# Rotated attention scores as products over 64 rows, one head in each half of the array

## The chip, the cores and the metric

The kernel runs on one core of a Trainium2 chip. The metric is the device time of one launch in microseconds; lower is better. The time before is the median of 3 runs, 2278.76 us (2278.57 to 2279.04).

## What is computed

A trunk of two layers over 256 tokens of width 2048, in float32: latent attention (MLA), a wide MLP, a state-space mixer (SSM), and a second MLP. The change lies in the attention scores. Each of the 16 heads has queries and keys of 192 numbers: 128 that are used as they are and 64 that are rotated by the token's position. The rotated part of the keys is the same for all heads up to a factor.

```
q = concatenate([q[..., :128], apply_rope(q[..., 128:], cos, sin)])
k = concatenate([k[..., :128], apply_rope(k[..., 128:], cos, sin)])
s = einsum('bqhd,bkhd->bhqk', q_blk, k) * 192 ** -0.5     # per block of 128 queries
p = softmax(where(k_pos <= q_pos, s, -inf))
o = einsum('bhqk,bkhd->bqhd', p, v)
```

So a score is a sum over 192 products: 128 of the unrotated part and 64 of the rotated one.

## The kernel before

**Stages.** `trunk` runs `mla`, `mlp`, `ssm`, `mlp` one after another. Nearly all of the time is projections: weights come from HBM in pieces of 128x1024 (queue of SP, line 85), ScalarE rounds a piece to float32r (L102), VectorE takes the rest (L103), and PE multiplies both halves (L340, L341, L344 in `block`; L619 to L621 in the MLPs). The weights are split three pieces ahead of PE.

**Units.** The 16 heads are worked on two at a time, in 8 units u. PE's order is the order of the calls in `mla_body` (PE alone is scheduled by hand; the other engines' order is set by a planner when the kernel is built). For each u, in that order:

- `s0q(u+1)`: the projection to the queries of the next unit
- `s1(u-1, "k")`: the normed keys of the unit before, transposed by PE (L940, L942) into two banks, then copied out into `kT`
- `s0kv(u)`: the projection to keys and values, with `s3(u-2)` in the middle, which transposes the softmax's result
- `s2(u-1)`: the scores of both heads (PE, L964 and L965), the masked copy with the maximum (VectorE, L968), the exponentials (ScalarE, L974), and the division
- `s4(u-2)`: scores times values (L1000, L1001), split by ScalarE and VectorE (L300, L301)
- `s1(u, "q")`: the normed queries, transposed into `qT`

In the last units the output projection (`wob`) takes the place of the projections that are not left.

**The layout of the scores' operands.** `kT` has three slabs of 128 rows: the unrotated keys of head 0, of head 1, and in slab 2 the rotated keys of head 0 in rows 0 to 63 and of head 1 in rows 64 to 127. `qT` has four: slabs 0 and 1 are the unrotated queries, slab 2 holds head 0's rotated queries in rows 0 to 63 with zeros below, slab 3 head 1's in rows 64 to 127 with zeros above. POOL writes the zeros (L930, L931), ScalarE the halves (L947). With the zeros, a product over all 128 rows of slab 2 of `kT` picks out one head.

**The scores.** Per head there are two blocks of queries: the first 128 queries against 128 keys, the other 128 against 256. Each is one product with the unrotated slab (L964) and one with the rotated slab (L965), summed in PSUM, in columns 0 to 127 and 128 to 383 of one bank per head. Plain float32 products run as two passes on PE, each with a weight load of its own.

**Banks.** `bank()` hands out four PSUM banks in rotation (two of pool `yp`, two of pool `sm`); a bank is written again when its readers are done.

**POOL** also computes the roots of the norms (L290, L291), the rotation (L801 to L804) and issues a copying DMA (L900).

Of the kernel before, what the change touches and what calls it, by code (L numbers as in the profile page):

```python
# [28 lines left out]
P = 128  # L29
# [186 lines left out]
class Trunk:  # L216
# [612 lines left out]
    def mla_body(self, mp, gain):  # L829
        nc, d = self.nc, self.d  # L830
# [93 lines left out]
        def s1(u, name):  # L924


            src, words = U[u][name + "n"], U[u].get(name + "w")
            dst = self.ktile(self.xtp, F32)
            if name == "q":
                nc.gpsimd.memset(dst[64:128, 2], 0.0)  # L930
                nc.gpsimd.memset(dst[0:64, 3], 0.0)  # L931
            for i in range(2):
                b = self.bank()
                parts = 2 - i
                for j in range(parts):
                    for t in range(2):
                        o = j * 256 + t * P
                        k = (2 * i + j) * P
                        if words is not None and (i, t) != (1, 1):
                            nc.tensor.transpose(b.bitcast(F32R)[:, o:o + P], words[:, t, k:k + P], self.ident_r)  # L940
                        else:
                            nc.tensor.transpose(b[:, o:o + P], src[:, t, k:k + P], self.ident)  # L942
                v = b[:, :parts * 256].rearrange("p (k n) -> p k n", k=parts)
                if i and name == "q":
                    for h in range(2):
                        r = slice(64 * h, 64 * h + 64)
                        nc.scalar.activation(dst[r, 2 + h], b[r, 0:256], AF.Copy)  # L947
                elif (i == 0) == (name == "q"):
                    nc.vector.tensor_copy(dst[:, 2 * i:2 * i + parts], v)
                else:  # L950
                    nc.scalar.activation(dst[:, 2 * i:2 * i + parts], v, AF.Copy)
            U[u][name + "T"] = dst

        def s2(u):
            qT, kT = U[u]["qT"], U[u]["kT"]
            p = self.ktile(self.xtp, F32).rearrange("p a b -> p (a b)")
            mx, nm, sm, rc = self.stat(4), self.stat(4), self.stat(4), self.stat(4)
            spans = ((0, P), (P, 384))
            for h in range(2):
                b = self.bank()  # L960
                q0, q1 = qT[:, h], qT[:, 2 + h]
                k0, k1 = kT[:, h], kT[:, 2]
                for o, n in ((0, P), (P, 256)):
                    nc.tensor.matmul(b[:, o:o + n], q0[:, o:o + P], k0[:, :n], start=True, stop=False)  # L964
                    nc.tensor.matmul(b[:, o:o + n], q1[:, o:o + P], k1[:, :n], start=False, stop=True)  # L965
                for i, (a, z) in enumerate(spans):
                    j = 2 * h + i
                    nc.vector.tensor_tensor_reduce(p[:, h * 384 + a:h * 384 + z], b[:, a:z], mk[:, 256 - (z - a):], 1.0, -3.0e38,  # L968
                                                   ALU.add, ALU.max, mx[:, j:j + 1])
                nc.vector.tensor_scalar(nm[:, 2 * h:2 * h + 2], mx[:, 2 * h:2 * h + 2], -SCALE, None, ALU.mult)  # L970
                for i, (a, z) in enumerate(spans):
                    j = 2 * h + i
                    v = p[:, h * 384 + a:h * 384 + z]
                    nc.scalar.activation(v, v, AF.Exp, bias=nm[:, j:j + 1], scale=SCALE, accum_out=sm[:, j:j + 1])  # L974
                nc.vector.reciprocal(rc[:, 2 * h:2 * h + 2], sm[:, 2 * h:2 * h + 2])
                for i, (a, z) in enumerate(spans):
                    j = 2 * h + i
                    nc.vector.tensor_scalar(p[:, h * 384 + a:h * 384 + z], p[:, h * 384 + a:h * 384 + z], rc[:, j:j + 1],
                                            None, ALU.mult)
            U[u]["p"] = p  # L980
# [40 lines left out]
        for u in range(UNITS):  # L1021
            if 0 < u and u + 1 < UNITS:
                s0q(u + 1)
                q_stats(u + 1)
            if u == UNITS - 1:
                a0 = wob(0, 0)
            if u >= 1:
                s1(u - 1, "k")
            if 0 < u and u + 1 < UNITS:
                q_norm(u + 1)  # L1030
            s0kv(u, (lambda: s3(u - 2)) if u >= 2 else None)
            if u + 1 < UNITS:
                q_rope(u + 1, self.pow.ins)
            if u == UNITS - 1:
                k_norm(u)
            if u >= 1:
                s2(u - 1)
            if u >= 2:
                s4(u - 2)
            s1(u, "q")  # L1040
            if u < UNITS - 1:
                k_norm(u)
        self.boundary_begin(gain, True)
        a1 = wob(1, 0)
        s1(UNITS - 1, "k")
        s3(UNITS - 2)
        wob(0, 1, a0)
        s4(UNITS - 2)
        s2(UNITS - 1)
        wob(1, 1, a1)  # L1050
        s3(UNITS - 1)
# [758 lines left out]
```

## Time and profile before

| | before |
|---|---|
| median of 3 runs | 2278.76 us |
| the profiled execution, its own time | 2280.22 us |
| its span, first to last instruction | 2278.4 us |
| PE busy | 2267.4 us |
| VectorE (DVE) busy | 1965.4 us |
| ScalarE (ACT) busy | 1441.1 us |
| GpSimd (POOL) busy | 285.1 us |
| granted TensorE clock | 1.00 |

The span is shorter than the execution's own time by 1.8 us of start and end. PE's matmuls are pipelined: a row's length holds the tail of a pass that overlaps the next one, so what a pass costs is the distance from its start to the next start. Attention takes the span from about 0 to 280 us; the eight units lie between about 66 and 212 us.

### The profile page before, as it was taken

How to read it: one execution, taken by the hardware profiler on the slowest of the kernel's cores; microseconds unless marked ns; L12 is line 12 of the kernel's file. 1: busy time of each engine (PE TensorE's matmuls, PEld its weight loads, DVE VectorE, ACT ScalarE, POOL GpSimd, SP SyncE). 2: the span in 40 equal slices, each digit the busy share in tenths (PEclk: the TensorE clock that was granted, in tenths of full speed). 3: DMA queues.
4: the chain of work that ended last, by engine and by line, in shares of the span. 5: the costliest groups of instructions: out<-in, count | busy, mean ns of one | idle time of the engine just before them, and what ended most of it. 6: DMA issues, size and time to landing. Idle time of an engine off the chain costs nothing.

```text
span 2278.4 us, 30856 instructions
## 1 busy us (share of the span) xinstructions
PE 2267.4 (100%) x10881; PEld 1880.1 (83%) x10881; DVE 1965.4 (86%) x2257; ACT 1441.1 (63%) x2044; POOL 285.1 (13%) x339
## 2 busy tenths in 40 slices
PE   9999999999999999999999999999999999999999
PEld 7898888888888888888888788888888888887887
DVE  7786697998999897879989998976989989989985
ACT  6775476566666566566677676565666665665663
POOL 1440000000000000100002532230000000000000
PEclk9999999999999999999999999999999999999999
DMA  8545678888888877768898889877788888898875
GB/s 316 174 153 151 218 229 264 255 260 267 265 254 262 270 240 241 237 195 260 274 366 285 291 293 330 268 227 221 219 256 251 258 275 244 259 280 238 265 230 162
DMA packets 176026, 569.74 MB, mean 250 GB/s; under 512 B 20192, under 2 KB 29344, under 8 KB 175872
## 3 DMA queue, kind: packets, MB, share of 16 engines
q1 hardware_dynamic: 147808, 498.24, 65.2%
q0 software_dynamic: 16320, 56.88, 11.7%
q10 hardware_dynamic: 11744, 12.66, 1.8%
q8 instruction: 85, 1.39, 0.2%
q14 instruction: 69, 0.57, 0.1%
HBM read 542.23 MB, written 6.41 MB: 241 GB/s over the span
## 4 chain that ended last, share of the span: by engine, by line
PE 94%; DVE 2%; DMA 2%; ACT 1%; issue 1%; POOL 0%; SPq 0%; ACTq 0%; DVEq 0%
PE acc L340 11%; PE acc L341 11%; PE acc L344 11%; PE yp L621 9%; PE yp L620 9%; PE yp L619 9%; PE st L620 7%; PE st L621 7%; PE st L619 7%; DMA wraw<-mi 1%; PE st L1162 1%; PE st L1163 1%; PE st L1164 1%; DVE wl L103 1%; PE yp L340 1%; PE yp L341 1%
## 5 line engine op out<-in xcount | busy, mean ns | idle before, releaser
L102 ACT ACTIVATE wh<-wraw 128x1024 fp32r<-128x1024 f32 (+1 forms) x818 | 857.4, 1053 | 526.3 <-PE acc L341 187.4
L103 DVE TENSOR_TENSOR wl<-wraw,wh 128x1024 fp32r<-128x1024 f32 (+1 forms) x818 | 989.1, 1227 | 180.2 <-ACT wh L102 171.0
L619 PE MATMUL yp<-wh,k 128*128 128x512 f32 x896 | 349.3, 390 | 0.0
L621 PE MATMUL yp<-wh,k 128*128 128x512 f32 x896 | 348.8, 389 | 0.0
L620 PE MATMUL yp<-wl,k 128*128 128x512 f32 x896 | 348.6, 389 | 0.0
L102 ACT ACTIVATE wh<-wrx 128x1024 fp32r<-128x1024 f32 x192 | 203.2, 1058 | 167.6 <-PE yp L621 104.4
L103 DVE TENSOR_TENSOR wl<-wrx,wh 128x1024 fp32r<-128x1024 f32 x192 | 233.6, 1222 | 39.4 <-ACT wh L102 37.6
L621 PEld LDWEIGHTS yp<-wh,k 128*128 128x128 f32 x896 | 168.2, 188 | 35.1
L620 PEld LDWEIGHTS yp<-wl,k 128*128 128x128 f32 x896 | 168.2, 188 | 34.9
L619 PEld LDWEIGHTS yp<-wh,k 128*128 128x128 f32 x896 | 168.2, 188 | 34.8
L340 PE MATMUL acc<-wh,k 128*128 128x512 f32 x496 | 196.4, 396 | 0.0
L341 PE MATMUL acc<-wh,k 128*128 128x512 f32 x496 | 193.4, 390 | 0.0
L340 PE MATMUL acc<-wh,xt 128*128 128x512 f32 x480 | 191.8, 400 | 1.2 <-ACT wh L102 1.2
L341 PE MATMUL acc<-wh,xt 128*128 128x512 f32 x480 | 187.4, 390 | 0.5 <-DVE xt L484 0.4
L619 PE MATMUL st<-wh,xt 128*128 128x512 f32 x448 | 177.7, 397 | 0.0
L621 PE MATMUL st<-wh,xt 128*128 128x512 f32 x448 | 174.9, 390 | 0.0
L620 PE MATMUL st<-wl,xt 128*128 128x512 f32 x448 | 174.7, 390 | 0.0
L200 POOL DMA_DIRECT2D wrx<-mi x56 | 49.0, 875 | 724.3 <-DVE wl L103 513.4
L619 PE MATMUL st<-wh,sN 128*128 128x512 f32 x336 | 133.2, 396 | 0.4 <-ACT wh L102 0.4
L620 PE MATMUL st<-wl,sN 128*128 128x512 f32 x336 | 131.5, 391 | 1.9 <-DVE wl L103 1.8
L344 PE MATMUL acc<-wl,k 128*128 128x512 f32 x496 | 132.7, 389 | 0.0
L621 PE MATMUL st<-wh,sN 128*128 128x512 f32 x336 | 131.1, 390 | 0.0
(342 smaller groups left out, 3808.6 us busy)
## 6 DMA issues: line engine op xcount, KB each, us to landing
wraw<-mi SPq DMA_DIRECT2D x256, 512.0 KB, 5.6
wraw<-mo SPq DMA_DIRECT2D x256, 512.0 KB, 5.4
wraw<-si SPq DMA_DIRECT2D x160, 512.0 KB, 6.0
wraw<-so SPq DMA_DIRECT2D x64, 512.0 KB, 4.9
wrx<-mi SPq DMA_DIRECT2D x56, 512.0 KB, 5.2
wrx<-mi POOLq DMA_DIRECT2D x56, 512.0 KB, 7.5
wraw<-wo SPq DMA_DIRECT2D x32, 512.0 KB, 4.0
tap<-xD SPq DMA_DIRECT2D x24, 512.0 KB, 8.1
```

Of the source, the lines that this page charges most:

```text
L102: self.last = nc.scalar.activation(h[:, v], raw[:, v], AF.Copy)
L103: self.last_lo = nc.vector.tensor_tensor(lo[:, v], raw[:, v], h[:, v].bitcast(F32), ALU.subtract)
L200: nc.gpsimd.dma_start(st["b11"].tile, quarter(d, 1, 0), accum_op=ALU.add)
L340: nc.tensor.matmul(accs[t][:, :n], ah, wh[:, q, :], start=first and kt + q == 0, stop=False)
L341: nc.tensor.matmul(accs[t][:, :n], al, wh[:, q, :], start=False, stop=False)
L344: nc.tensor.matmul(accs[t][:, :n], lhs(kt + q, t)[0], wl[:, q, :], start=False, stop=en and q == nk - 1)
L619: nc.tensor.matmul(b, ah, wh, start=first and q == 0, stop=False)
L620: nc.tensor.matmul(b, ah, wl, start=False, stop=False)
L621: nc.tensor.matmul(b, al, wh, start=False, stop=last and q == 1)
L1162: nc.tensor.matmul(bank[onto], ah, wh, start=done + q == 0 and not skip, stop=False, skip_group_check=skip)
L1163: nc.tensor.matmul(bank[onto], al, wh, start=False, stop=False, skip_group_check=skip)
L1164: nc.tensor.matmul(bank[onto], ah, wl, start=False, stop=done == 3 and q == 1, skip_group_check=skip)
```

## The change

The zeros go, and with them the two memsets. Slabs 2 and 3 of `qT` are still there, but only the half with numbers in it is written and read. Both banks are taken first. PE then computes the unrotated products of head 0 and head 1 (two blocks each), and after them the rotated ones as products over 64 rows: head 0 over rows 0 to 63, head 1 over rows 64 to 127, in turn, first for the short block and then for the long one, added to what the bank holds. Since both blocks of a head are open in one bank at the same time, only the first product into a bank is marked as a start. What follows on the other engines is written as before, in a loop of its own after all eight products.

```diff
             dst = self.ktile(self.xtp, F32)
-            if name == "q":
-                nc.gpsimd.memset(dst[64:128, 2], 0.0)
-                nc.gpsimd.memset(dst[0:64, 3], 0.0)
             for i in range(2):
...
             spans = ((0, P), (P, 384))
-            for h in range(2):
-                b = self.bank()
-                q0, q1 = qT[:, h], qT[:, 2 + h]
-                k0, k1 = kT[:, h], kT[:, 2]
-                for o, n in ((0, P), (P, 256)):
-                    nc.tensor.matmul(b[:, o:o + n], q0[:, o:o + P], k0[:, :n], start=True, stop=False)
-                    nc.tensor.matmul(b[:, o:o + n], q1[:, o:o + P], k1[:, :n], start=False, stop=True)
+            banks = [self.bank() for _ in range(2)]
+            parts = ((0, P), (P, 256))
+            for h, b in enumerate(banks):
+                for o, n in parts:
+                    nc.tensor.matmul(b[:, o:o + n], qT[:, h, o:o + P], kT[:, h, :n], start=o == 0, stop=False, skip_group_check=True)
+            for o, n in parts:
+                for h, b in enumerate(banks):
+                    r = slice(64 * h, 64 * h + 64)
+                    nc.tensor.matmul(b[:, o:o + n], qT[r, 2 + h, o:o + P], kT[r, 2, :n], start=False, stop=True, skip_group_check=True)
+            for h, b in enumerate(banks):
                 for i, (a, z) in enumerate(spans):
```

## The prediction

> **What bounds the kernel now.** I read the page's first part, then the chain that ended last, then PE's waits in the attention stage, and last the order of time around one unit's scores. The engine line and the chain:
>
> ```profile
> PE 2267.4 (100%) x10881; PEld 1880.1 (83%) x10881; DVE 1965.4 (86%) x2257; ACT 1441.1 (63%) x2044; POOL 285.1 (13%) x339
> PE 94%; DVE 2%; DMA 2%; ACT 1%; issue 1%; POOL 0%; SPq 0%; ACTq 0%; DVEq 0%
> ```
>
> PE is the bound, and 94% of the chain runs through it. So time taken from PE's own stream counts in full unless PE then waits for something else. PE's waits between 57 and 230 us, where the change lies, are two:
>
> ```profile
> PE yp L942 <- ACT xt L947: 0.5, 1, 0.5
> PE yp L942 <- DVE qn L890: 0.4, 1, 0.4
> ```
>
> The score products (L964, the unrotated part, and L965, the rotated part) take the following time. Each stretch runs from the first score pass of a unit to the first pass of what follows; the columns are the stretch, its length, then the busy times of L964 alone. The eight lengths (shown: the first, the last and the sum) are the cost of all score products:
>
> ```profile
> 83.60:86.20 2.60, 1.96 (x8) 1.18 (x7) 1.00 0.62 207
> 195.25:197.87 2.62, 1.96 (x8) 1.18 (x8) 1.00 0.67 195
> sum 20.94, PE 15.69 PEld 9.41; mean PE 1.96 PEld 1.18
> ```
>
> One unit in order of time (the third, u = 2; a row is a start, a length with the pipelined tail in it, and a count of passes, so costs are read from start to start):
>
> ```profile
> 113.98 0.38 PE L964 MATMUL sm<-xt,xt 128*128 128x128 f32 x2
> 114.20 0.39 PE L965 MATMUL sm<-xt,xt 128*128 128x128 f32 x2
> 114.42 0.60 PE L964 MATMUL sm<-xt,xt 128*128 128x256 f32 x2
> 114.86 0.59 PE L965 MATMUL sm<-xt,xt 128*128 128x256 f32 x2
> 115.29 0.38 PE L964 MATMUL yp<-xt,xt 128*128 128x128 f32 x2
> ...
> 116.17 0.59 PE L965 MATMUL yp<-xt,xt 128*128 128x256 f32 x2
> 116.60 0.59 PE L1000 MATMUL sm<-xt,v 128*128 128x256 f32 x2
> ```
>
> Every fp32 product is two passes (x2). A product over 128 columns costs 114.20 - 113.98 = 0.22 us, that is 0.11 a pass; one over 256 columns 0.44, 0.22 a pass. A head costs 1.31 (0.22 + 0.22 + 0.44 + 0.43), a unit 2.62. Half of it, 1.31, is L965; that half is 128 rows tall of which 64 are zeros.
>
> **The change, part by part.**
>
> *1. Eight products a unit, as before.* Four L964 products keep their form, 1.31 us. The rotated parts become four products of 64 rows, head 0 in rows 0 to 63 and head 1 in rows 64 to 127, each pair into two different banks. Alone, each costs as much as before, since time goes by moving columns. They gain only where the two halves run side by side. The trace has no pair of row halves. The nearest rows are column halves: L1453 issues 64 passes over 64 columns to the two column halves in turn.
>
> ```profile
> 1216.03 0.61 PE L344 MATMUL acc<-wl,xt 128*128 128x512 f32 x2
> 1216.26 0.39 PE L344 MATMUL acc<-wl,xt 128*128 128x512 f32 x1
> 1216.58 0.28 PE L1453 MATMUL y<-xtm,mt 128*64 128x64 f32 x2
> 1216.58 2.08 PE L1453 MATMUL y<-xtm,mt 128*64 128x64 f32 x64
> 1218.20 0.46 PE L1453 MATMUL y<-xtm,mt 128*64 128x64 f32 x10
> 1218.59 0.50 PE L340 MATMUL acc<-wh,xt 128*128 128x512 f32 x1
> 1218.93 0.39 PE L341 MATMUL acc<-wh,xt 128*128 128x512 f32 x1
> 1219.16 0.40 PE L340 MATMUL acc<-wh,xt 128*128 128x512 f32 x1
> ```
>
> The first two passes start together (x2 in 0.28 us of length). The last ten begin at 1218.20, so the first 27 pairs took 1.62 us, 0.06 a pair. One pass of 64 columns alone must cost about 0.055 (half of the 0.11 above): two ran for the price of one. I take this for the row halves: the rotated part falls from 1.31 to 0.65 us, 0.65 saved a unit, 5.2 in all. That is the upper end of what PE can save here; the lower end is nothing, if row halves take turns.
>
> *2. Two changes of array shape a unit.* The same rows price them. Going in: L344's pass at 1216.26 should be followed 0.23 later (1216.26 - 1216.03), and L1453 starts 0.32 later: 0.09 lost. The first pair then costs 0.05 more than the others (1.62 - 27 x 0.058), as its weights could not be loaded ahead: 64 columns of weights; the scores have 128, so 0.10. Going out: ten passes from 1218.20 end at 1218.49, and L340 starts at 1218.59: 0.10 lost. L341 follows 0.34 later instead of 0.23: 0.11, again an unhidden load of 128 columns. Together 0.40 a unit. A 64-row shape stands in the trace once, without a partner:
>
> ```profile
> 1026.93 0.84 PE L344 MATMUL yp<-wl,xt 128*128 128x512 f32 x3
> 1027.71 0.34 PE L1293 MATMUL sm<-ident,s 64*128 64x64 f32 x2
> 1027.97 0.43 PE L1294 MATMUL sm<-dt,tri 128*128 128x64 f32 x2
> ```
>
> The third L344 pass lies 2 x 0.23 after 1026.93, at 1027.39, and L1293 follows 0.32 later: the same 0.09 for a row shape. Bounds for this term: 0.20 if the loads hide after all, 0.51 if the two halves' first loads take turns (0.11 more). I take 0.40.
>
> The Trainium skill, TensorEngine Tiling (Array Packing), section Key Properties, says that a change of tiling mode, not just of tile, drains the TensorE. The rows agree (0.09 in, 0.10 out); without that rule the sum would be the 5.2 us of part 1, with it 2.0.
>
> Net on PE: 0.65 - 0.40 = 0.25 a unit, 2.0 us for eight.
>
> *3. Later scores for head 0, earlier for head 1.* Now head 0's bank is complete 1.31 us after the start and head 1's after 2.62. After the change both are complete after about 1.31 + 0.19 + 0.65 = 2.15. VectorE reads them here (unit 2, started at 113.98):
>
> ```profile
> 115.30 1.22 DVE L103 TENSOR_TENSOR wl<-wraw,wh 128x1024 fp32r<-128x1024 f32 x1
> 116.44 0.29 DVE L968 CUSTOM_DVE_ANT_0 xt<-sm,mk 128x128 f32<-128x128 f32 x1
> 118.57 0.28 DVE L968 CUSTOM_DVE_ANT_0 xt<-yp,mk 128x128 f32<-128x128 f32 x1
> 119.76 0.90 DVE L970 TENSOR_SCALAR st<-st 128x2 f32<-128x2 f32 x1
> 122.19 0.69 DVE L301 TENSOR_TENSOR k<-sm,k 128x512 fp32r<-128x512 f32 x1 [0.32 <-ACT k L300]
> ```
>
> It comes to head 0 at 2.46 and to head 1 at 4.59, since a weight split (L103) is ahead of it. So head 0's delay is hidden: cost 0. Without that cover (the last unit, where L968 follows PE closely) head 0's chain starts some 0.8 later and head 1's 0.5 earlier. Behind that wait on VectorE stand weight splits that PE needs three pieces later: 0 again, since a piece there is 12 passes of 0.23, or 2.7 us of PE.
>
> *4. The chain that ends at the next unit's keys.* Who is late next once PE is shorter? After s4's product, ScalarE and VectorE split the output (L300, L301), behind the exponentials in their queues, and the second bank of the next key transposes (L942) reuses that bank. Units 1 and 2:
>
> ```profile
> 106.86 0.69 DVE L301 TENSOR_TENSOR k<-yp,k 128x512 fp32r<-128x512 f32 x1 [0.31 <-ACT k L300]
> 107.54 0.44 PE L942 MATMUL yp<-ident,kn 128*128 128x128 f32 x2 [0.54 <-ACT xt L947]
> 123.03 0.38 PE L942 MATMUL sm<-ident,kn 128*128 128x128 f32 x2
> ```
>
> In unit 1 PE starts at 107.54, when L301 ends (107.55): it has stalled already, about 0.7 us by starts. In unit 2 L301 ends at 122.88, and PE starts at 123.03: 0.15 to spare. So unit 1's saving of 0.25 would only lengthen a stall, unless the chain gets shorter too, and unit 2's is cut to 0.15.
>
> *5. The memsets.* Sixteen of about 0.3 us leave POOL, which is 13% busy: nothing by themselves. But one sits ahead of L804:
>
> ```profile
> 118.75 0.45 POOL L803 TENSOR_TENSOR rb<-qn,ss 128x128 f32<-128x128 f32 x1
> 119.27 0.31 POOL L930 MEMSET xt<- 64x256 f32 x1
> 119.65 0.73 POOL L804 TENSOR_TENSOR qn<-ra,rb 128x256 f32<-128x256 f32 x1
> ```
>
> L804 runs to 120.38, and VectorE's tiny L970 in the chain of part 4 (2 numbers a row) takes 0.90 us from 119.76, ending only after it; with POOL idle, in the last unit, it takes 0.17:
>
> ```profile
> 197.44 0.17 DVE L970 TENSOR_SCALAR st<-st 128x2 f32<-128x2 f32 x1
> ```
>
> With the memset gone, L804 starts about 0.4 earlier, so L970 and the chain end 0.3 to 0.4 earlier. That gives back unit 2's margin and takes about 0.3 from unit 1's stall. Bounds: 0 if the other engines are ordered anew and the overlap falls elsewhere, 0.7 if the stall goes altogether.
>
> No DMA is added, removed or moved; the same loads stand in SP's queue, and POOL's own DMA (L900) comes a little earlier. The second bank is written 0.65 us sooner than now; its last reader in the rotation of four banks was in the key transposes, a whole projection before, so no new wait.
>
> **Sum.** Seven units at 0.25 = 1.75, and 0.3 in unit 1: 2.05, say 2.0 us less. The profiled execution took 2280.22 us (span 2278.4 and 1.8 around it), so 2278.2; it stands 1.5 above the median 2278.76, so the median should come to 2276.8. That is 0.09%, inside the 0.2% (4.6 us) which is about what a measurement can tell from no change.
>
> **The rivals.**
>
> *A. The row halves take turns.* The place is the two rotated pairs; the price is the shape change of 0.40 a unit and no gain, 3.2 us. PE then comes to unit 1's bank 0.4 later, the chain 0.3 earlier, and the stall of 0.7 goes: 2.5 net, 2281.3, slower than before. It decides as soon as overlap saves less than 0.40 of the 0.65. For it: no row of this trace shows two row halves together. Against it: column halves of the same fp32 form do overlap.
>
> *B. The passes stagger.* If a half's two passes must go one after the other and the next half waits behind them, only the second pass of one meets the first of the next: 0.11 + 0.11 + 0.22 + 0.22 + 0.22 = 0.88 in place of 0.65. That saves 0.43, less 0.40, so 0.03 a unit and, with unit 1's 0.3, 2278.2: no change. Against it: L1453's first two passes started together, though each product there too is two passes. The Trainium skill, TensorE: Matmul & The Clock Gate, section The mechanism, says that matmuls start and end in strict program order, which would give this case if the two passes are two instructions in that order; the rows of L1453 do not look so.
>
> *C. The shape changes hide, and the stall goes.* 5.2 + 0.7 = 5.9, so 2272.9, faster by 0.26%. Against it: all L1453 rows pay the change, and so does L1293.
>
> *D. The order of the other engines is planned anew,* and weight splits fall behind L968's later wait. PE's longest single wait for a split elsewhere is in this row; once a unit it would be 6.4 us, so 2283 to 2285.
>
> ```profile
> PE st L620 <- DVE wl L103: 1.8, 3, 0.8
> ```
>
> Against it: VectorE is busy 12.13 of 15 us in this stage (the third busy column of the stretch below), and only one group of PE's instructions changes.
>
> ```profile
> 110.00:125.00 15.00, 15.00 (x90) 13.70 (x89) 12.13 (x37) 11.13 (x39) 6.81 (x11) 1.00 0.47 150
> ```
>
> **How the numbers follow.** Forecast 0.62, A 0.14, B 0.14, C 0.04, D 0.06. Faster by over 0.2% is C and a sliver of the forecast: 0.05. Slower by over 0.2% is D and the bad end of A: 0.07. The rest, 0.88, is no change. The range goes from 2274.8 (loads hidden: 8 x 0.45, and half the stall, 4.0) to 2281.6 (A with a little more); the forecast's own is 2275.6 to 2278.0.
>
> **What would show it.** Right: the rotated passes appear as 64*128, in pairs that start together; a unit's stretch from first score pass to the pass after it is about 2.25 us and not 2.62, and the pass after it is about 0.1 longer; L942's wait in unit 1 is shorter. Wrong: stretches of 2.8 (A) or 2.5 (B) us, of 2.0 (C), or new PE waits for L103 between 80 and 210 us (D).

## The result and the profile after

| | before | after |
|---|---|---|
| median (21 runs each, alternating) | 2279.37 us | 2283.43 us |
| lowest to highest | 2277.24 to 2283.37 us | 2280.73 to 2288.34 us |
| the profiled execution, its own time | 2280.22 us | 2280.73 us |
| its span | 2278.4 us | 2279.0 us |
| PE busy | 2267.4 us | 2266.9 us |

The ratio is 1.0015 (95%: 1.0009 to 1.0022): 4.1 us slower by medians, where 2 us less were forecast, and above the end of the range (2281.6). The two profiled executions differ by only 0.5 us. To read that, one needs to know that 18 of the 21 runs of the changed kernel had a mean granted clock of 0.999 or 0.998 (medians 2283.73 and 2284.07) and three, one of them the profiled one, had 1.000 (median 2281.39). So there are two losses to find: about 1.5 us that the runs at full clock have (2281.39 against about 2279.9, the old kernel's median over its 62 runs at clock 1.000 beside the experiments), and 2.3 us more with the lower clock. The first rests on three runs and the traces below.

The first two lines that the prediction showed of before look much the same:

```profile
PE 2266.9 (99%) x10881; PEld 1875.2 (82%) x10881; DVE 1961.6 (86%) x2257; ACT 1441.4 (63%) x2044; POOL 282.2 (12%) x323
PE 93%; DVE 3%; DMA 2%; ACT 1%; issue 1%; POOL 0%; SPq 0%; ACTq 0%; POOLq 0%; DVEq 0%
```

In the rows of after, L960 are the unrotated products (before: L964), L964 the rotated ones (L965), L937 and L939 the transposes (L940, L942); L968 is the masked copy in both. Unit 1 on PE, in order of time:

```profile
97.05 0.81 PE L960 MATMUL yp<-xt,xt 128*128 128x128 f32 x4
97.70 0.82 PE L960 MATMUL sm<-xt,xt 128*128 128x128 f32 x4
98.45 0.37 PE L964 MATMUL yp<-xt,xt 64*128 64x128 f32 x1
98.45 0.37 PE L964 MATMUL sm<-xt,xt 64*128 64x128 f32 x1
98.66 0.27 PE L964 MATMUL yp<-xt,xt 64*128 64x128 f32 x1
98.67 0.27 PE L964 MATMUL sm<-xt,xt 64*128 64x128 f32 x1
...
98.99 0.38 PE L964 MATMUL yp<-xt,xt 64*128 64x256 f32 x1
...
99.30 0.70 PE L1000 MATMUL yp<-xt,v 128*128 128x256 f32 x2
99.84 0.38 PE L1001 MATMUL yp<-xt,v 128*128 128x128 f32 x2
...
100.63 0.54 PE L937 MATMUL sm<-ident,qw 128*128 128x128 f32 x4
103.56 0.28 PE L937 MATMUL yp<-ident,qw 128*128 128x128 f32 x1 [2.39 <-DVE st L968]
```

Two things are to be seen. The rotated passes are `64*128` and start in pairs within 0.01 us: the scores take 2.25 us (97.05 to 99.30) and no longer 2.62. And the last row has a wait that was not there: PE stands 2.39 us until VectorE's masked copy (L968) gives a bank free. In the view of waits between 57 and 230 us, PE's two largest, and those of the weight load that goes ahead of each pass (the columns are total, times, longest):

```profile
PE yp L937 <- DVE st L968: 2.4, 1, 2.4
PE sm L937 <- DVE st L968: 0.5, 1, 0.5
```

```profile
PEld yp L937 <- DVE st L968: 3.1, 3, 2.5
PEld sm L937 <- DVE st L968: 1.1, 3, 0.6
```

The weight load waits for L968 six times, 4.2 us in all; before, neither it nor a pass waited for L968. The stall of 0.5 that the prediction quoted at L942 in unit 1 has gone in turn. Why the bank is late stands in VectorE's rows of unit 1, first after, then before:

```profile
98.55 2.35 DVE L103 TENSOR_TENSOR wl<-wraw,wh 128x1024 fp32r<-128x1024 f32 x2
102.08 0.87 DVE L919 SCALAR_TENSOR_TENSOR kn<-acc,st,cst 128x128 f32<-128x128 f32 x3 [1.18 <-POOL st L291]
102.87 0.28 DVE L968 CUSTOM_DVE_ANT_0 xt<-yp,mk 128x128 f32<-128x128 f32 x1
...
103.07 0.42 DVE L968 CUSTOM_DVE_ANT_0 xt<-yp,mk 128x256 f32<-128x256 f32 x1
...
103.63 0.17 DVE L970 TENSOR_SCALAR st<-st 128x2 f32<-128x2 f32 x1
```

```profile
98.83 2.35 DVE L103 TENSOR_TENSOR wl<-wraw,wh 128x1024 fp32r<-128x1024 f32 x2
101.09 0.28 DVE L968 CUSTOM_DVE_ANT_0 xt<-yp,mk 128x128 f32<-128x128 f32 x1
...
101.30 0.42 DVE L968 CUSTOM_DVE_ANT_0 xt<-yp,mk 128x256 f32<-128x256 f32 x1
...
102.35 0.35 DVE L919 SCALAR_TENSOR_TENSOR kn<-acc,st,cst 128x128 f32<-128x128 f32 x1 [0.63 <-POOL st L291]
```

VectorE's order has changed. Before, head 0's masked copy came right behind the weight splits, and the key norms (L919), which wait for a root from POOL (L291), came behind it. After, three key norms stand ahead of the copy: VectorE idles 1.18 us for the root, then works on them for 0.8, and the copy starts at 102.87 in place of 101.09, though the scores are done 1.1 us sooner (99.30 against 100.41). The second bank of `s1(u, "q")`, four banks on in the rotation, is head 0's score bank. PE reached it here in the old kernel:

```profile
102.02 0.24 PE L940 MATMUL yp<-ident,qw 128*128 128x128 f32 x1
```

The copy had read its last at 101.72 (101.30 + 0.42): 0.3 us to spare.

The other units wait less, but they too lose what they gained. From a unit's first score pass to its first transpose into that second bank the old kernel takes 4.23 us in unit 2 (113.98 in the prediction's rows, to 118.21), and the same in units 1 and 3 to 5. The changed one takes 6.51 in unit 1 (97.05 to 103.56), and in unit 2 4.26:

```profile
114.81 0.82 PE L960 MATMUL sm<-xt,xt 128*128 128x128 f32 x4
...
119.07 0.28 PE L937 MATMUL sm<-ident,qw 128*128 128x128 f32 x1
```

Units 3 to 5 take 4.24 to 4.27: a wait of about 0.3 eats the 0.25 that the products save there.

How far the program has come is easily compared at the first transposes behind attention (L325; the columns to read are the start and end of the four passes), before and after:

```profile
L325 PE MATMUL yp<-ident,s x4: 270/272/272, 278.5 to 278.8; 128*128 128x128 f32 x4
```

```profile
L325 PE MATMUL yp<-ident,s x4: 270/272/272, 279.7 to 280.0; 128*128 128x128 f32 x4
```

At the end of attention the changed kernel is 1.2 us behind, in a profile without any loss of clock. But it was 0.4 ahead at the first score pass (83.19 against 83.60), before the change can act. From that pass to the L325 row it takes 196.5 us and the old kernel 194.9: 1.6 more, which fits the 1.5 of the runs at full clock. PE's products alone would have made it about 2 us less.

### The profile page after: what moved, and what is told of

Read it like the earlier page. It is cut to its first block, busy times and chain, and to the rows that moved or that the text cites. A ratio compares the mean times of both kernels' runs of the same rounds, so it can differ in the third digit from the quotient of the medians.

```text
span 2279.0 us, 30820 instructions
## 1 busy us (share of the span) xinstructions
PE 2266.9 (99%) x10881; PEld 1875.2 (82%) x10881; DVE 1961.6 (86%) x2257; ACT 1441.4 (63%) x2044; POOL 282.2 (12%) x323
## 4 chain that ended last, share of the span: by engine, by line
PE 93%; DVE 3%; DMA 2%; ACT 1%; issue 1%; POOL 0%; SPq 0%; ACTq 0%; POOLq 0%; DVEq 0%
PE acc L340 11%; PE acc L341 10%; PE acc L344 10%; PE yp L621 9%; PE yp L619 9%; PE yp L620 9%; PE st L620 7%; PE st L621 7%; PE st L619 7%; DVE wl L103 1%; DMA wraw<-mi 1%; PE st L1162 1%; PE st L1164 1%; PE st L1163 1%; PE yp L340 1%; PE yp L341 1%
## 5 line engine op out<-in xcount | busy, mean ns | idle before, releaser
L103 DVE TENSOR_TENSOR wl<-wraw,wh 128x1024 fp32r<-128x1024 f32 (+1 forms) x818 | 987.6, 1224 | 180.3 <-ACT wh L102 171.3
L103 DVE TENSOR_TENSOR wl<-wrx,wh 128x1024 fp32r<-128x1024 f32 x192 | 233.4, 1221 | 39.8 <-ACT wh L102 38.5
L344 PE MATMUL acc<-wl,k 128*128 128x512 f32 x496 | 132.7, 389 | 0.0
```

Source lines behind the costliest of these rows:

```text
L103: self.last_lo = nc.vector.tensor_tensor(lo[:, v], raw[:, v], h[:, v].bitcast(F32), ALU.subtract)
L344: nc.tensor.matmul(accs[t][:, :n], lhs(kt + q, t)[0], wl[:, q, :], start=False, stop=en and q == nk - 1)
```

## The experiments

The theory: PE's part came as forecast, but VectorE's order was planned anew around the later first bank, so that the query transposes wait for the bank that L968 reads. Rivals: the cost lies in the row halves themselves, in the absence of the memsets, or in the runs' clock alone. Every kernel ran beside the old one: r1 to r4 on one chip, r5 to r8 on a second, r9 to r11 on a third. "End of attention" is the start of the L325 row in its profile. The profiles reach the first score pass at 82.4 to 83.6 us, so the column behind it, the distance from that pass to the end of attention, is the better one to compare. It is 194.9 for the old kernel and 196.5 for the changed one; in r2, r3 and r8 it holds 1.7 us of lost clock (see r2).

| run | kernel | median | before beside it | ratio (95%) | end of attention | from the first score pass |
|---|---|---|---|---|---|---|
| r1 | changed, key norms put behind the copies | 2279.46 | 2280.38 | 0.9997 (0.9988 to 1.0006) | 277.1 | 193.9 |
| r2 | old, key norms put ahead of the copies | 2286.22 | 2280.38 | 1.0022 (1.0012 to 1.0031) | 283.1 | 200.4 |
| r3 | changed order of products, 128 rows with zeros | 2283.05 | 2280.38 | 1.0012 (1.0004 to 1.0021) | 281.5 | 198.4 |
| r4 | changed, again | 2283.86 | 2280.38 | 1.0014 (1.0005 to 1.0023) | 280.1 | 196.5 |
| r5 | changed, eight idle passes one turn ahead of the wait | 2281.14 | 2280.44 | 1.0004 (0.9996 to 1.0013) | 278.7 | 196.3 |
| r6 | changed, query transposes later | 2279.38 | 2280.44 | 0.9992 (0.9983 to 1.0000) | 275.6 | 192.9 |
| r7 | old, query transposes later | 2280.35 | 2280.44 | 0.9998 (0.9989 to 1.0006) | 277.7 | 194.4 |
| r8 | changed, memsets kept | 2283.10 | 2280.44 | 1.0016 (1.0008 to 1.0025) | 281.6 | 198.2 |
| r9 | r6 and r1 together | 2277.42 | 2280.76 | 0.9989 (0.9980 to 0.9998) | 275.6 | 192.5 |
| r10 | r6, one half's four passes, then the other's | 2278.51 | 2280.76 | 0.9993 (0.9984 to 1.0002) | 275.5 | 192.6 |
| r11 | r6, again | 2278.81 | 2280.76 | 0.9992 (0.9983 to 1.0000) | 276.0 | 193.0 |

**r1: the order put back.** The key norms are told to VectorE's planner behind the last masked copy:

```diff
-                    nc.vector.tensor_tensor_reduce(p[...], b[:, a:z], ...)
+                    self.masked = nc.vector.tensor_tensor_reduce(p[...], b[:, a:z], ...)
...
                 s2(u - 1)
+            if u < UNITS - 1:
+                with self.tc.issue_after(self.masked.ins) if u else nullcontext():
+                    k_norm(u)
...
-            if u < UNITS - 1:
-                k_norm(u)
```

> The changed kernel with one thing more: VectorE's key norms (L919) may not be issued before the masked copies (L968) of both heads. Theory W (the planner put two key norms, which wait for POOL's root, ahead of the masked copies; the query transposes wait for the bank): PE's waits for L968 fall from about 3 us to under 0.3, and the 2.0 us predicted for PE come out: 0.997 to 0.9995 of before, some 2276.5 to 2278.5, granted clock 1.000 in the profile and in the timed runs. Rival C (the eight units of row halves, with their two drains each, lower the granted clock in the timed runs): the waits go, but the timed runs stay 2 to 4 us above before at a clock of 0.998 to 0.999.

The ratio falls from 1.0014 (r4, beside it) to 0.9997, not quite to the 0.9995 expected. Part of the wait stays, where under 0.3 was expected:

```profile
PE yp L937 <- DVE st L968: 1.0, 1, 1.0
PE sm L937 <- DVE st L968: 0.5, 1, 0.5
```

The planner put a third weight split ahead of the copy in unit 1, so this is not the old order exactly. The clock was 1.000 in 8 of 11 runs (median 2278.91), in the changed kernel in 3 of 21.

**r2: the order alone, on the old kernel.** Products, banks, zeros and memsets stay as they were; only the planner is given the key norms first:

```diff
+            if 0 < u < UNITS - 1:
+                k_norm(u)
             if u >= 1:
-                s2(u - 1)
+                with self.tc.issue_after(self.normed.ins) if u < UNITS - 1 else nullcontext():
+                    s2(u - 1)
+            if u == 0:
+                k_norm(u)
...
-            if u < UNITS - 1:
-                k_norm(u)
```

> The kernel before, products of 128 rows and zeros kept, with all four key norms (L919) issued ahead of the masked copies, so later than in the changed kernel. Theory W: PE waits for L968 in unit 1 by 2 us or more and in unit 6 by some 0.3 to 0.6, gains back the 0.7 us stall: span 1.5 to 4 us above before, ratio 1.0006 to 1.002. Rival C: no row halves, so clock 1.000 and the time of before within 1 us.

It made the old kernel slower by a factor of 1.0022, 5.8 us by medians, a little more than the 1.002 expected. All four key norms stand ahead of the copy here, in the changed kernel three. The wait appears in the same place, at the old kernel's transposes:

```profile
PE yp L940 <- DVE st L968: 3.1, 2, 2.8
```

So the order by itself is enough for a loss of this kind, with no row halves at all. The wait also brings something that no step of the prediction held. In stretches of this profile (the columns are the stretch, its length, busy times of PE, its weight load, VectorE, ScalarE and POOL, then the granted clock):

```profile
99.00:103.00 4.00, 2.29 (x16) 1.97 (x14) 2.82 (x5) 0.92 (x4) 3.92 (x4) 1.00 0.75 215
103.00:106.00 3.00, 1.94 (x10) 1.92 (x11) 2.93 (x15) 1.72 (x9) 2.53 (x6) 0.86 0.40 151
106.00:109.00 3.00, 3.00 (x12) 3.00 (x11) 2.19 (x7) 2.51 (x7) 0.25 (x1) 0.57 0.33 131
```

Just after PE has stood still, the clock falls: the last stretch has 12 passes, where the changed kernel's profile, at full clock, has 21 (shown under r8). 0.86 and 0.57 over 3 us each are 1.7 us of lost clock, that is 3.4 us at half speed (each 3 us times what is missing from 1, over 0.5). The same profile has a second such stretch, 3.4 us from 1265.7 on, in the state-space stage.

**r3: the new order of products without the row halves.** All 128 rows, zeros and memsets kept:

```diff
-                    r = slice(64 * h, 64 * h + 64)
+                    r = slice(0, P)
```

> The changed order of products (both heads' unrotated parts, then the rotated parts), but the rotated parts over all 128 rows with the zeros and memsets kept: no change of array shape, no pairs. Theory W: the late banks alone make the planner move the key norms ahead, so the same wait appears: about 2.3 us in unit 1 and little after, and PE has 2.62 us a unit again: 2 to 4 us slower than before, 1.001 to 1.0018. Rival C: time of before within 1 us at clock 1.000.

The scores take the old 2.62 us a unit here, and the kernel is slower by a factor of 1.0012. Three key norms stand ahead of the copy as in the changed kernel, and the wait is there too, if shorter (L971 here is L968 elsewhere). So the shape of the products is not what moves VectorE's order:

```profile
PE yp L940 <- DVE st L971: 1.8, 1, 1.8
```

What is left are two things that r3 shares with the changed kernel: head 0's bank completes later, and the copies are written in a loop of their own after all eight products. No run holds these two apart.

**r4: the changed kernel once more,** beside r1 to r3.

> The changed kernel as it is, beside the others on one chip, to see its clock and its waits again. Theory W: wait of 2.4 us in unit 1 in the profile; timed runs 1 to 4 us above before. Rival C: its timed runs alone show a granted clock under 1.000.

1.0014, with the same two waits of 2.4 and 0.5 us, and a clock of 0.999 in 8 of 11 runs (median 2284.28); the profiled run, at 1.000, took 2281.37.

**r5: idle passes ahead of the wait.** Eight passes of 512 columns that nobody reads:

```diff
+                if (u, name, i) == (1, "q", 0):
+                    for _ in range(8):
+                        nc.tensor.matmul(b, self.ident_r, cq[0].rearrange("p a b -> p (a b)")[:, :512], start=True, stop=True)
```

> The changed kernel with eight idle passes of 512 columns (1.8 us of PE work whose result is overwritten) in front of the query transposes of unit 1, where PE waits 2.4 us for the bank. Theory W2 (besides its own length, the wait halves PE's clock for one window of 3.4 us in most timed runs, since PE was idle too long): the wait in the trace shrinks to about 0.6 us, the span stays within 0.5 us of the changed kernel's profile, and the timed runs fall by 1.5 to 2.5 us to some 2281.5 to 2282.5, with far more of them at clock 1.000. Rival C2 (the clock drops come from elsewhere, such as the row halves or the state-space stage): the timed runs stay at 2283.5 to 2284, mostly at 0.999.

The passes do not stand where PE waits. `u` in the edit is the turn of the loop, and turn 1 has unit 0's scores and, behind them, the query transposes of unit 1. The long wait comes one turn later, behind unit 1's scores. In r5's rows on PE (L940 are the query transposes here):

```profile
84.67 2.14 PE L933 MATMUL yp<-cq,ident 128*128 128x512 f32 x8
...
102.63 0.28 PE L940 MATMUL yp<-ident,qw 128*128 128x128 f32 x1 [0.34 <-DVE st L971]
```

So PE is held up with work one unit early, comes 1.9 us later to unit 1's scores (98.17 - 82.41 against 97.05 - 83.19), and waits 0.34 there in place of 2.39. Work has taken the place of idle time all the same: from the first score pass to the end of attention it takes 196.3 us, the changed kernel 196.5. The median is 2281.14, ratio 1.0004 against 1.0014 to 1.0016 without; the clock was 1.000 in 6 of 11 runs, against 3 of 11 in r4. That is what a clock that follows PE's idle time would give. But it is not a clean test: VectorE's order in unit 1 moved with it (two weight splits ahead of the copy in place of three), and the six runs at full clock have a median of 2280.23, 1.1 under r4's, for which the traces show no reason. The span, expected within 0.5 us of the changed kernel's, is 2.1 shorter, of which 0.8 stood already at the first score pass.

**r6 and r7: the query transposes later.** Instead of mending VectorE's order, PE comes later to the bank: `s1(u, "q")` moves behind the next unit's query projection, once on the changed kernel (r6) and once on the old one (r7).

```diff
             s0q(u + 1)
             if u >= 1:
+                s1(u - 1, "q")
                 s1(u - 1, "k")
...
-            s1(u, "q")
+            if u == UNITS - 1:
+                s1(u, "q")
```

> The changed kernel with PE's query transposes moved behind the next query projection, some 8 us after the scores, so that no bank is waited for whatever order VectorE has. Theory W: PE's waits for the masked copies are gone although two key norms still stand ahead of them; span 2.5 to 4 us below before (2.0 from the row halves, up to 0.7 from the stall in unit 1, up to 0.8 from the wait at the first query transposes); timed ratio 0.9982 to 0.9992. Rival (the pairs of row halves gain less than the start times show): no more than 1 us below before.

> The kernel before with the same move of the query transposes, full height and zeros. It is the partner of the run with the row halves: theory W has the two differ by 2.0 us (0.25 a unit) in the span; this one lies 0.5 to 1.5 us below before. Rival: the two differ by under 0.5 us.

In r6 VectorE still has three key norms ahead of the copy and still idles 1.18 us for POOL's root, but PE no longer stands:

```profile
PE sm L937 <- DVE st L968: 0.5, 1, 0.5
PE yp L939 <- DVE kn L919: 0.3, 1, 0.3
```

The 0.5 is behind unit 6's scores, in the last turn of the loop, whose query transposes were not moved. r6 gives 0.9992, r7 0.9998. r6's span is 1.4 us below the old kernel's profile, where 2.5 to 4 were expected; r7's median is 0.1 below its neighbours, where 0.5 to 1.5 were. With the waits out of the way in both, the pair also shows what the row halves are worth. First r6, then r7:

```profile
L325 PE MATMUL yp<-ident,s x4: 270/272/273, 275.6 to 275.9; 128*128 128x128 f32 x4
```

```profile
L325 PE MATMUL yp<-ident,s x4: 270/272/273, 277.7 to 278.0; 128*128 128x128 f32 x4
```

r6 is 2.1 us ahead, of which 0.7 already stood at 15 us, before the first score; 1.4 grew over the units, about 0.2 for each, where 2.0 were expected. By medians it is 1.0 (2279.38 against 2280.35). r7's profiled run itself took 2283.94: it met a stretch of half clock at about 1260 us, in the state-space stage, during a wait of 3.1 us that PE has there; the old kernel's profile has one of 1.3 at that place.

**r8: the memsets kept** in the changed kernel:

```diff
+            if name == "q":
+                nc.gpsimd.memset(dst[64:128, 2], 0.0)
+                nc.gpsimd.memset(dst[0:64, 3], 0.0)
```

> The changed kernel with the sixteen memsets put back (their zeros are not read by the products over 64 rows). If the planner's new order comes from the score banks and not from the memsets, VectorE still has two key norms ahead of the masked copies, PE waits 1.5 to 2.5 us in unit 1, and the time is that of the changed kernel within 1 us. If the memsets' removal made the new order, the waits are gone and the time is 1 to 3 us below before.

1.0016, with waits of 2.4 and 0.5 us as in the changed kernel. So the memsets' absence costs nothing, and their presence saves nothing. This run shows the second loss best, since it has the same wait and its profiled execution caught the clock. First r8, then the changed kernel, at the same places:

```profile
99.00:103.00 4.00, 2.42 (x20) 1.85 (x16) 2.82 (x5) 0.93 (x5) 3.92 (x3) 1.00 0.73 217
103.00:106.00 3.00, 2.14 (x12) 2.14 (x13) 2.96 (x16) 2.32 (x11) 2.58 (x6) 0.89 0.38 147
106.00:109.00 3.00, 3.00 (x12) 3.00 (x11) 2.32 (x6) 1.97 (x4) 0.34 (x1) 0.54 0.33 131
```

```profile
99.00:103.00 4.00, 2.17 (x16) 1.63 (x12) 2.82 (x6) 0.97 (x5) 3.92 (x4) 1.00 0.83 215
103.00:106.00 3.00, 2.44 (x15) 2.44 (x16) 2.85 (x16) 2.32 (x10) 1.94 (x4) 1.00 0.46 182
106.00:109.00 3.00, 3.00 (x21) 2.92 (x20) 2.41 (x5) 2.94 (x9) 0.00 (x0) 1.00 0.26 102
```

Both stand still in the first stretch. In r8 the clock then falls to 0.89 and 0.54, in the changed kernel's profile it stays at 1.00; PE gets through 12 passes in the last stretch in the one and 21 in the other. From the first score pass to the end of attention r8 takes 198.2 us, the changed kernel 196.5: the 1.7 us of lost clock.

**r9: both remedies.** r6 with r1's order. It is the version that the rest pointed to:

> The changed kernel with the query transposes moved behind the next query projection, and VectorE's key norms kept behind the masked copies as well. Theory W: the last wait for a bank (0.5 us in the unit before the last, whose query transposes could not be moved) falls to under 0.2, span 0.3 to 1 us below the run with the move alone, timed ratio to before 0.998 to 0.9995. Rival: the key norms, now later, hold up the next key transposes and the time rises by 0.5 us or more.

0.9989 (0.9980 to 0.9998): faster than the old kernel by 3.3 us and, over their own neighbours, than the changed one by 0.25%. Against r11, the move alone on the same chip, it is 0.5 us ahead in attention (192.5 against 193.0) and 1.4 by medians; the intervals of their ratios overlap, so what VectorE's order adds to the move is not shown. The clock was 1.000 in 8 of 11 runs. In VectorE's rows of unit 1 the copies now come right behind the weight splits, and the key norms after them:

```profile
97.43 2.35 DVE L103 TENSOR_TENSOR wl<-wraw,wh 128x1024 fp32r<-128x1024 f32 x2
99.69 0.28 DVE L968 CUSTOM_DVE_ANT_0 xt<-yp,mk 128x128 f32<-128x128 f32 x1
...
100.95 0.35 DVE L919 SCALAR_TENSOR_TENSOR kn<-acc,st,cst 128x128 f32<-128x128 f32 x1
```

The wait of 0.5 behind unit 6's scores stayed, which I had expected to fall below 0.2: there the query transposes keep their old place, close behind the scores.

**r10 and r11: one half after the other, and r6 again.** In r10 the four rotated passes of one head are issued first, then the four of the other:

```diff
-            for o, n in parts:
-                for h, b in enumerate(banks):
+            for h, b in enumerate(banks):
+                for o, n in parts:
```

> The changed kernel with the query transposes moved, and the products over 64 rows issued head by head (all four passes of rows 0 to 63, then all four of rows 64 to 127) rather than in turn. If only neighbours in PE's queue can run side by side, the halves take turns: a unit's rotated part is 1.31 us and not 0.65, 0.65 a unit more and 4 to 5.2 us in the span. If the queue reaches four passes ahead into the other half of the array, nothing changes: pairs start within 0.01 us of each other and the span is that of the run in turn within 0.5 us.

> The changed kernel with the query transposes moved, again, as the partner of the two others on one chip: 2 to 4 us below before, span near 2277.

0.9993 against 0.9992: no loss. (r11's median is 1.95 us below its neighbours and its span 2277.5, where 2 to 4 and some 2277 were expected.) The rows of r10's unit 1 say why; in the program the four `yp` passes stand ahead of the four `sm` passes:

```profile
98.22 0.37 PE L964 MATMUL yp<-xt,xt 64*128 64x128 f32 x1
98.23 0.37 PE L964 MATMUL sm<-xt,xt 64*128 64x128 f32 x1
...
98.77 0.38 PE L964 MATMUL sm<-xt,xt 64*128 64x256 f32 x1
99.08 0.70 PE L1000 MATMUL yp<-xt,v 128*128 128x256 f32 x2
```

The halves run side by side all the same: the unit takes 2.26 us (96.82, its first score pass, to 99.08) and not the 2.9 that turns would cost (2.26 and 0.65 more). The Trainium skill, TensorE: Matmul & The Clock Gate, section The mechanism, says that matmuls start and end in strict program order; these rows differ, as those of L1453 in the old kernel did.

## Why the prediction was wrong, step by step

**Right: the row halves (part 1).** Pairs start together, 0.65 saved. Rivals A and B, a unit of 2.8 or 2.5 us, did not come; it is 2.25. One of the prediction's readings was too long, though nothing hangs on it: in the first and the last unit the pass behind the scores starts 2.43 us after their first (86.03 and 197.68), not 2.60 and 2.62.

**Right: the two changes of shape (part 2).** Taken at 0.40; the rows of unit 1 give 0.39. Going in, L964 starts 0.75 after 97.70 where the four unrotated passes before it took 0.66 in the old kernel (half of a head's 1.31): 0.09. The first pair takes 0.21 (98.45 to 98.66) for 0.11: 0.10. Going out, 0.31 (98.99 to 99.30) for 0.22: 0.09. L1000 then takes 0.54 (to 99.84) for 0.43 (the old kernel's rows have 0.43 between such starts): 0.11. Net 0.26 a unit, about 2.0 us for eight, as forecast. Of these, r6 against r7 measured 1.4 in the traces and 1.0 by medians.

**Wrong: part 3, "head 0's delay is hidden: cost 0".** This step took VectorE's order as given and asked only when it would come to the bank. In the changed kernel the planner put three key norms in front of the masked copy, and these wait for a root from POOL. The step followed what stands behind L968 on VectorE (weight splits), and not who waits for the bank that L968 reads: the second query-transposes bank, with 0.3 us to spare. (Part 5 did ask of the banks, but only whom the second score bank waits for: "so no new wait".) What the term of 0 measured: 4.2 us in six waits (2.5 of it in unit 1). Less the 2.0 of the products and the old stall of about 0.7 that gives 1.5 us, near the 1.6 of the trace and the loss of the runs at full clock. r2 shows the order alone at work; r3 shows that a wait of that kind comes without row halves; r1 takes most of it away by the order, r6 by PE's, r9 by both, and the loss goes with it. Part 5's "0 if the other engines are ordered anew" had the new order in its words but gave it a price of nothing; it was not free.

**Rival D** was given 0.06, with 2283 to 2285 us. The time is in it, and the order of the engines as well, but its place and mechanism are not: in this stage no pass waited for L103 (one weight load did, for 0.3), weight splits did not fall behind L968, and the argument against it ("only one group of PE's instructions changes") did not hold: VectorE's order changed all the same. Its price was misread too: PE's longest single wait for a split in the old trace is not 0.8 but 1.3 (L344, at about 1259 us).

**Not in the prediction at all: the clock.** After such a wait PE ran at half clock for 3.4 us in r2, r3 and r8. That would account for 1.7 us (r8's stretches) of the 2.3 by which the two groups of runs differ. The five sets of runs with a wait of 1.8 us or more in unit 1 (the changed kernel's 21, r2, r3, r4, r8) had a mean clock of 1.000 in 14 of 65 runs, the seven others in 48 of 77, the old kernel in 62 of 94. In the changed kernel itself the fall is inferred: both of its profiles were at 1.000, so it stands in the traces of r2, r3 and r8 and, for the changed kernel, only in the mean clock of its other runs.

**Parts 4 and 5: not borne out.** L942's old stall in unit 1 is gone, but PE now stands before that, so the 0.3 counted as gain cannot be told apart in the balance above. Part 5 gave a memset as the reason for L970's 0.90 us, because it pushes L804 under it. L970 does take 0.17 now (the row at 103.63 above), but L804 runs beside it all the same:

```profile
103.65 0.74 POOL L804 TENSOR_TENSOR qn<-ra,rb 128x256 f32<-128x256 f32 x1
```

And in r8 and r3, with the memsets, it takes 0.16 and 0.17 too; in r7, with the memsets and VectorE's old order, 0.9. So the short L970 came with VectorE's new order and not with the memsets' absence; why it is short stays open.

**Open.** What in the planner's reckoning moved the key norms is not known: that it goes by when a bank is ready fits r3, but so does a planner that goes by where the copies stand in the program. Open too are the first 83 us, where the profiles already differ by up to 1.2 us, and the 0.7 us that the changed kernel's profile wins back between the end of attention (1.2 behind) and its end (0.5).

## What to carry to other kernels

When a planner orders the other engines, a change to one engine's products can move whole groups of the others' instructions; "hidden" then needs the next writer of that buffer and its spare time (here 0.3 us, in plain sight in the old trace), not only the reader's. The products did get their 2 us shorter; to collect some of it (1.0 us by medians, 1.4 in the traces, r6 against r7), the query transposes had to be put one projection later, where the banks are free. A distance within the trace, from the first place that the change touches, held to 0.1 us between two executions of the same kernel (196.5 twice; 192.9 and 193.0), where the time since the start differed by 0.4. And a single profile, here one at full clock, can stand to the median as 0.5 us does to 4.

## What the runs showed of the hardware that was not expected

- Waits of 1.8 to 2.8 us on PE were followed by a granted clock of half, 1 to 1.5 us after work had begun again, for 3.4 us (r2 after 2.8, r8 after 2.4, r3 after 1.8). It does not come in every execution: the changed kernel's two profiles have a wait of 2.4 and no fall. The old kernel has a mean clock of 0.999 in 32 of 94 runs, which is what one such stretch would give (1.7 us of 2280); where it lies in them is not on record, but in the profiles of r7 and r2 one lay in the state-space stage, at 1260 and 1266 us.
- How the wait lies to windows of 3.413 us seems to decide. In every profile the clock changes only at whole multiples of that time after its first record in the trace (4.4 to 7.6 us into the execution): in r8 29 of them later, at 105.32, in r7 367 of them, at 1260.26. The window just before r8's fall, and the one that fell:

```profile
101.91:105.32 3.41, 1.46 (x9) 1.46 (x10) 2.93 (x16) 2.25 (x10) 3.04 (x6) 1.00 0.62 217
105.32:108.73 3.41, 3.41 (x13) 3.41 (x12) 2.71 (x9) 2.65 (x8) 0.98 (x3) 0.50 0.29 115
```

PE stood still for 1.95 of the 3.41 us there. In the windows before the other falls, that at the program's end aside, it was 1.76 and 2.32 (r2), 1.85 (r3) and 2.07 (r7). r3's wait of 1.8 lay whole in one window; that of 2.4 in the changed kernel's second profile (r4) was cut into 1.54 and 0.83, and no fall came. The border is not sharp in these traces: 1.90 in the changed kernel's first profile and 1.79 in r11's brought none. The Trainium skill, TensorE: Matmul & The Clock Gate, section What's actually happening, states that the clock is halved after at least one idle window of about 3.4 us, with a window that runs freely. The length of the slow stretch and its coming and going agree; the idle time that was enough here is shorter.

- Products in the two row halves overlap even when one half's four passes stand in the program wholly ahead of the other's (r10): the second half's first pass starts 0.01 us after the first half's. To alternate them in the code brought nothing.
